# A decoder layer on one core: other column cuts for the last output tile, and other engines for two of four modulation sums

## The chip, the cores and the metric

One core of one Trainium2 chip runs the program; the seven others are idle. The metric is the device time of one execution in microseconds, lower is better. Five engines work side by side, each through its own instructions in order: TensorE (PE in the profile, PEld for its weight loads), VectorE (DVE), ScalarE (ACT), GpSimd (POOL) and SyncE (SP, which here only issues DMAs). They wait for each other through semaphores.

## The reference

A layer over 256 tokens of width 1024, batch 1. What matters here is its first and its last step:

```python
mod = c @ w_ada[layer] + b_ada[layer]
shift, scale, gate = jnp.split(mod, 3, axis=-1)
h = x * (1.0 + scale[:, None, :]) + shift[:, None, :]
proj = h @ w_in[layer]
...
y = jnp.concatenate([o_a, o_b], axis=-1) @ w_out[layer]
x = _layernorm(DEEPNORM_ALPHA * x + gate[:, None, :] * y, ln_g[layer], ln_b[layer])
```

`c` is one vector of 1024, `w_ada` is 1024 x 3072, `w_in` 1024 x 4096, `w_out` 1024 x 1024, all float32. Between the two steps lie two kinds of attention over eight heads each, each gated by a SiLU branch.

## The kernel before

**How the order comes about.** The kernel first records operations (`op`, with engine, assumed duration, what is read and written) in a plan. `Plan.emit` then plays the plan forward with its assumed costs, and each engine takes whatever is ready and due first. So the order on each engine is a result of the assumed durations, and an edit at one place can move instructions elsewhere. On the chip each engine keeps that order and waits wherever an operand is late.

**The modulation (`modulate`, lines 393 to 443).** `mod = c @ w_ada` needs, for each of 2048 columns (shift and scale; gate is made later), a sum over 1024 rows of `w_ada`. The rows are laid out as 128 partitions times eight rows j, so the work is first eight weighted additions, acc = acc + c[j] * row j, over 512 columns each, and then one sum across the partitions. The columns come in four pairs g = 0 to 3 (`GROUPS`); pair g gives shift and scale of the x tiles 2g and 2g + 1, tile k being 128 of the 1024 features. The kernel before does this in three ways:

- Pair 0: all eight additions on VectorE (lines 412 and 415), then the sum across partitions as matmuls of acc against a column of ones (line 423, two tiles times shift and scale, each of them in two passes), which leaves the result in the wanted layout.
- Pairs 1 and 2 (`pag=[1, 2]`): rows 0 to 3 go through TensorE, as products with `cz`, a tile that holds c[j] in one column of 32 (line 406, four products with 512 columns each, into one PSUM buffer). VectorE then adds rows 4 to 7, the first of them onto that PSUM buffer. The sum across partitions is a product with 32 columns of ones (line 432), a COPY to SBUF by VectorE (line 436) and a transpose on TensorE (line 437).
- Pair 3: all eight additions on VectorE, then lines 432 to 437.

Two small additions of the bias give `md` (line 440), and `make_h` forms h = x * (1 + scale) + shift for the tile: `hH` is its high part in float32r, `hL` the rest (for the first tile of a pair `hH` comes from VectorE, line 450; for the second from ScalarE).

**The projections.** x is transposed on TensorE tile by tile (line 387) and copied out by ScalarE into `xT`. Each 128-row block of the weights is split into a high part (`whi`, ScalarE, line 270) and a low part (`wlo`, VectorE, line 275). A product is three matmuls: hH with whi, hL with whi, hH with wlo (line 296 is the helper that records nearly every matmul). `proj1(k)` does this for x tile k and the first 1792 columns of `w_in`: 36 matmuls, 30 of 256 and 6 of 512 columns. It can only begin when hH of tile k is there. Nine further sets of columns follow, with the attention in between.

**The output.** Products with `w_out` for token tile t go into PSUM pieces `CUTS[t]`: two of 512 columns for t = 0, and 512, 384 and 128 columns for t = 1. Each piece gets 24 matmuls (eight contraction blocks times three parts). Two of the eight blocks of t = 1 are done early, in a fill stretch (`fill`, nf = 2); the other six come piece by piece at the very end. `layer_norm(1)` follows: for each piece an addition of x (line 275) and statistics (line 743) on VectorE, then their aggregate, the power -0.5 on GpSimd, two normalising steps and three output DMAs.

**Loads.** SyncE issues all loads in the order of `LOADS`, through 11 raw buffers; the eight row blocks of a pair (a10 to a13 for pair 1) are eight DMAs.

Of the kernel before, what the change touches and what calls it, by code (L numbers as in the profile page):

```python
# [237 lines left out]
def hybrid_kernel(ctx: ExitStack, tc: tile.TileContext, x, c, w_in, w_out, w_ada, b_ada, ln_g, ln_b,  # L238
# [154 lines left out]
    md = {}  # L393

    def modulate(g):

        tiles = GROUPS[g]
        n = 128 * len(tiles)
        acc = P.buf("acc", [128, 2, n])
        a = [T["ada", g, j] for j in range(8)]  # L400
        d = 2 * n / 0.96 + 128
        if g in CFG["pag"]:

            pa = P.buf("ps", [128, 2, n])
            for j in range(4):
                pe(n * 0.977, lambda j=j: nc.tensor.matmul(  # L406
                    pa.ap[32 * j:32 * j + 32], cz[:, j], a[j][0](), start=True, stop=True, skip_group_check=True), a[j][1] + ["cz"], [(pa, 0)], 512)
            pe_end()
        for j in range(4 if g in CFG["pag"] else 0, 8):
            src, rd = a[j][0], a[j][1] + ["c"]  # L410
            if j == 0:
                op(DVE, n / 0.96 + 133, lambda src=src: nc.vector.tensor_scalar(acc.ap, src(), cc[:, 0:1], None, op0=OP.mult),
                   rd, [(acc, 0)], p2=True)
                continue
            op(DVE, d, lambda src=src, j=j: nc.vector.scalar_tensor_tensor(  # L415
                acc.ap, src(), cc[:, j:j + 1], pa.ap if j == 4 and g in CFG["pag"] else acc.ap, op0=OP.mult, op1=OP.add),
                rd + [(pa, 0) if j == 4 and g in CFG["pag"] else (acc, 0)], [(acc, 0)], p2=j > 4)
        if g not in CFG["colsum"]:
            pm = P.buf("ps", [128, len(tiles), 2])
            for q, k in enumerate(tiles):  # L420
                cs = slice(q * 128, q * 128 + 128)
                for s in range(2):
                    pe(205, lambda q=q, s=s, cs=cs: nc.tensor.matmul(pm.ap[:, q, s:s + 1], acc.ap[:, s, cs], ones[:, 0:1],  # L423
                       start=True, stop=True, skip_group_check=True), [(acc, 0)], [(pm, 1)], 4)
            pe_end()
            col = lambda q: pm.ap[:, q]
        else:

            pm, z = P.buf("ps", [128, 2, 128]), P.buf("md", [128, 128])
            for s in range(2):  # L430
                for q in range(2):
                    pe(50, lambda r=64 * s + 32 * q, s=s, cs=slice(q * 128, q * 128 + 128): nc.tensor.matmul(  # L432
                        pm.ap[r:r + 32, 0], ones[:, 0:32], acc.ap[:, s, cs], start=True, stop=True, skip_group_check=True),
                       [(acc, 0)], [(pm, 0)], 128)
# [523 lines left out]
```

## Time and profile before

| | us |
|---|---|
| three timed runs | 163.99, 164.50, 165.16 |
| median | 164.50 |
| the profiled execution | 164.21 |
| its span in the trace | 162.4 |
| TensorE busy | 152.6 |
| VectorE busy | 136.9 |
| ScalarE busy | 96.2 |

The profile is one execution. The span runs from the first to the last instruction that the trace holds; the profiled execution's own time is 1.8 us longer. A matmul's end in the trace is modelled and overlaps the next one, so its price is read from the distance between starts, not from its duration. A line in the code can be that of a helper: 270, 275 and 296 stand for many operations, which are told apart by the names of what they write and read. Times in views are counted from the start of the span.

### The profile page before, as it was taken

Reading aid. Unit: us, or ns where it says so; the run is one execution under the profiler, and the core shown is the slowest. Engines: PE = TensorE matmul, PEld = TensorE weight load, DVE = VectorE, ACT = ScalarE, POOL = GpSimd, SP = SyncE. Lnnn points to the kernel's source line nnn. Section 1 sums busy time; section 2 is a strip of 40 time slices with the busy share of each in tenths; the row PEclk is TensorE's granted clock in tenths of the full one; section 3 lists DMA queues with packets and bytes.
Section 4 is the critical chain, followed back from the end, with each engine's and each line's share of the span. In section 5 each row is a group of like instructions: output and inputs, shape, how many; then the busy total and the mean of one; then the engine's idle time right before and its main releaser. Section 6 shows DMA issues by size and latency. Waiting matters only on the chain.

```text
span 162.4 us, 3296 instructions
## 1 busy us (share of the span) xinstructions
PE 152.6 (94%) x1192; PEld 132.1 (81%) x1192; DVE 136.9 (84%) x313; ACT 96.2 (59%) x243; POOL 3.1 (2%) x9
## 2 busy tenths in 40 slices
PE   6998998999999999999999999999999999999920
PEld 2447976789988999997998999899799978888920
DVE  2687668686999979999999899999999999828672
ACT  3008608406788798447999999952589991503000
POOL 3000000000000000000000000000000000001020
PEclk9999999999999999999999999999999999999975
DMA  5999999999999999997457839700199700000303
GB/s 147 272 388 387 349 387 362 361 402 359 369 401 357 348 348 348 349 346 235 137 178 224 281 118 348 277 4 0 17 328 404 288 4 4 0 0 0 129 0 129
DMA packets 25405, 38.11 MB, mean 235 GB/s; under 512 B 1681, under 2 KB 20141, under 8 KB 25390
## 3 DMA queue, kind: packets, MB, share of 16 engines
q1 hardware_dynamic: 25066, 37.76, 68.0%
q8 instruction: 9, 0.15, 0.4%
q10 hardware_dynamic: 324, 0.15, 0.3%
q14 instruction: 6, 0.05, 0.1%
HBM read 36.85 MB, written 1.05 MB: 233 GB/s over the span
## 4 chain that ended last, share of the span: by engine, by line
PE 93%; DVE 3%; issue 1%; DVEq 0%
PE ps L296 79%; PE ps L792 6%; PE ps L677 3%; PE ps L387 1%; PE ps L406 1%; DVE raw L765 1%; PE ps L432 1%; PE ps L423 1%; DVE hH L450 1%; DVE raw L760 0%; DVE wlo L275 0%; PE ps L556 0%; DVE md L275 0%; DVEq L954 0%; DVE bn L743 0%
## 5 line engine op out<-in xcount | busy, mean ns | idle before, releaser
L270 ACT ACTIVATE whi<-raw 128x512 fp32r<-128x512 f32 (+1 forms) x83 | 45.8, 610 | 30.3 <-DMA raw<-in_w_in_dram 18.7
L275 DVE TENSOR_TENSOR wlo<-raw,whi 128x512 fp32r<-128x512 f32 (+1 forms) x83 | 51.6, 665 | 1.0 <-ACT whi L270 0.7
L296 PE MATMUL ps<-hH,whi 128*128 128x256 f32 x192 | 46.1, 290 | 1.4 <-DVE hH L450 1.3
L296 PE MATMUL ps<-hH,wlo 128*128 128x256 f32 x192 | 45.4, 285 | 0.0
L296 PE MATMUL ps<-hL,whi 128*128 128x256 f32 x192 | 44.7, 284 | 0.0
L296 PEld LDWEIGHTS ps<-hH,whi 128*128 128x128 f32 x192 | 33.2, 190 | 4.5 <-issue 2.3
L296 PEld LDWEIGHTS ps<-hH,wlo 128*128 128x128 f32 x192 | 33.4, 190 | 1.7 <-issue 1.0
L296 PEld LDWEIGHTS ps<-hL,whi 128*128 128x128 f32 x192 | 33.0, 190 | 1.0 <-issue 0.4
L415 DVE SCALAR_TENSOR_TENSOR acc<-raw,cc,acc 128x512 f32<-128x512 f32 x20 | 15.0, 752 | 2.0 <-DMA raw<-in_w_ada_dram 1.4
L296 PE MATMUL ps<-whi,hH 128*128 128x256 f32 (+1 forms) x48 | 15.8, 332 | 0.0
L296 PE MATMUL ps<-whi,hL 128*128 128x256 f32 (+1 forms) x48 | 15.3, 321 | 0.0
L657 ACT ACTIVATE prob<-z,st 128x128 f32<-128x128 f32 (+1 forms) x32 | 14.2, 448 | 1.8 <-DVE st L654 1.8
L296 PE MATMUL ps<-wlo,hH 128*128 128x256 f32 (+1 forms) x48 | 15.2, 320 | 0.0
L296 PE MATMUL ps<-whi,ogh 128*128 128x512 f32 (+2 forms) x40 | 14.4, 359 | 0.0
L296 PE MATMUL ps<-wlo,ogh 128*128 128x512 f32 (+2 forms) x40 | 14.3, 357 | 0.0
L296 PE MATMUL ps<-whi,ogl 128*128 128x512 f32 (+2 forms) x40 | 14.3, 356 | 0.0
L272 ACT ACTIVATE prob<-prob,st 128x128 f32<-128x128 f32 (+1 forms) x32 | 12.3, 444 | 0.4 <-DVE st L662 0.4
L548 DVE SCALAR_TENSOR_TENSOR gate<-raw,cc,gate 128x512 f32<-128x512 f32 x16 | 11.2, 739 | 0.7 <-DMA raw<-in_w_ada_dram 0.7
L792 PE MATMUL ps<-warm 128*128 128x512 bf16 x36 | 10.5, 446 | 1.3 <-DVE warm L311 1.3
L275 DVE TENSOR_TENSOR pp<-ps,rope_t 128x512 f32<-128x512 f32 x16 | 10.3, 682 | 1.1 <-PE ps L296 1.1
L296 PEld LDWEIGHTS ps<-whi,hH 128*128 128x128 f32 x48 | 9.0, 190 | 1.1 <-issue 0.7
L270 ACT ACTIVATE pt<-ps 128x384 f32<-128x384 f32 x16 | 7.4, 487 | 3.6 <-PE ps L677 3.5
(84 smaller groups left out, 184.2 us busy)
## 6 DMA issues: line engine op xcount, KB each, us to landing
raw<-in_w_in_dram SPq DMA_DIRECT2D x26, 512.0 KB, 8.0
raw<-in_w_ada_dram SPq DMA_DIRECT2D x32, 256.0 KB, 7.2
raw<-in_w_ada_dram SPq DMA_DIRECT2D x8, 512.0 KB, 4.5
raw<-in_w_out_dram SPq DMA_DIRECT2D x8, 512.0 KB, 7.6
raw<-in_w_in_dram SPq DMA_DIRECT2D x8, 384.0 KB, 7.5
out_dram<-raw SPq DMA_DIRECT2D x3, 256.0 KB, 2.0
xs<-in_x_dram SPq DMA_DIRECT2D x1, 512.0 KB, 6.7
gate<-gate_row SPq DMA_DIRECT2D x1, 512.0 KB, 4.4
```

The source lines that it names most:

```text
L270: op(ACT, dur, lambda: nc.scalar.activation(o(), i(), AF.Copy), r, w)
L272: op(ACT, dur, lambda: nc.scalar.activation(o(), i(), AF.Copy, scale=scale()), r, w)
L275: op(e, dur, lambda: vec[e].tensor_tensor(o(), a(), b(), alu), r, w, p2=p2)
L296: f = lambda: nc.tensor.matmul(o(), a(), b(), start=start, stop=stop, skip_group_check=True)
L387: pe(107, lambda t=t: nc.tensor.transpose(b.ap[:, t * 128:(t + 1) * 128], xs[:, t, k * 128:(k + 1) * 128], ident), [("x", 0 if k == 0 else ...
L406: pe(n * 0.977, lambda j=j: nc.tensor.matmul(pa.ap[32 * j:32 * j + 32], cz[:, j], a[j][0](), start=True, stop=True, skip_group_check=True) ...
L415: op(DVE, d, lambda src=src, j=j: nc.vector.scalar_tensor_tensor(acc.ap, src(), cc[:, j:j + 1], pa.ap if j == 4 and g in CFG["pag"] else a ...
L423: pe(205, lambda q=q, s=s, cs=cs: nc.tensor.matmul(pm.ap[:, q, s:s + 1], acc.ap[:, s, cs], ones[:, 0:1], start=True, stop=True, skip_group ...
L548: op(DVE, 663, lambda cs=cs: nc.vector.scalar_tensor_tensor(gate[:, cs], b.ap[:, cs], cc[:, r:r + 1], gate[:, cs], op0=OP.mult, op1=OP.add ...
L657: op(ACT, n * 0.833 + 280, lambda e=e, t=t, i=i, c=c: nc.scalar.activation(p[e].ap[:, c], z[e].ap[:, c], AF.Exp, bias=st.ap[:, i:i + 1], s ...
L677: pe(109, lambda i=i: nc.tensor.transpose(b.ap[:, i * 128:(i + 1) * 128], p.ap[:, i * 128:(i + 1) * 128], ident), [(p, 1 if i else 0)], [( ...
L792: op(PE, 216, lambda: nc.tensor.matmul(pw.ap, warm[:, 0:128], warm, start=True, stop=True), [], [(pw, 0)], due=1e8)
```

## The change

Three edits, and what the planner makes of them.

1. Token tile 1's output is cut into 512, 256 and 256 columns. The planner's assumed cost of a narrow matmul gets a floor of 112 ns.
2. Pairs 0 and 1 (`one=[0, 1]`): the eighth addition is done in two halves, one for each x tile, and the matmuls with the column of ones of a tile wait for their half alone. Pair 1 now takes the way of pair 0: all eight additions on VectorE and no products with `cz`.
3. Only pair 2 keeps products on TensorE, for rows 2 to 5 (`PROWS`). Their PSUM buffer is no longer added to by VectorE: ScalarE copies it to SBUF (`pas`), VectorE adds rows 0, 1, 6 and 7 by itself, and the products with ones take in both tiles, eight in place of four, accumulating in PSUM.

```diff
-CFG = dict(colsum=[1, 2, 3], pag=[1, 2], ...
+PROWS = (2, 3, 4, 5)
+CFG = dict(one=[0, 1], colsum=[2, 3], pag=[2], ...
...
+        rows = [j for j in range(8) if g not in CFG["pag"] or j not in PROWS]
+        def on_pe():
             pa = P.buf("ps", [128, 2, n])
-            for j in range(4):
+            for i, j in enumerate(PROWS):
...
+            o = P.buf("pas", [128, 2, n])
+            copy(lambda: o.ap, lambda: pa.ap, acost(512, True), [(pa, 0)], [(o, 0)])
+            return o
...
+            parts = [(q, slice(q * 128, q * 128 + 128)) for q in range(2)] if j == 7 and g in CFG["one"] else [(None, slice(0, n))]
+            for q, cs in parts:
...
+            if j == 1 and g in CFG["pag"]:
+                sums = [(on_pe(), 0)] + sums
...
-                       start=True, stop=True, skip_group_check=True), [(acc, 0)], [(pm, 1)], 4)
-            pe_end()
+                       start=True, stop=True, skip_group_check=True), [(acc, q)], [(pm, q)], 4)
+                if q or g in CFG["one"]:
+                    pe_end()
...
-            for s in range(2):
+            for i, (x, _) in enumerate(sums):
+                for s in range(2):
...
-    CUTS = (((0, 512), (512, 1024)), ((0, 512), (512, 896), (896, 1024)))
+    CUTS = (((0, 512), (512, 1024)), ((0, 512), (512, 768), (768, 1024)))
...
-                mm((c1 - c0) / 2.2 + 2, [(o, i), (w, c0 // 512), "late"], [(b, 0)], lambda b=b: b.ap,
+                mm(max((c1 - c0) / 2.2 + 2, 112), [(o, i), (w, c0 // 512), "late"], [(b, 0)], lambda b=b: b.ap,
```

VectorE around pair 1, before. `acc` is the running sum, `raw` the loaded rows, `ps_315` the products with cz, `wlo` low parts of weights, and the hH that ends the piece is that of x tile 2.

```order
L275 TENSOR_TENSOR wlo_276<-raw_148,whi_267 128x512 x2
L275 TENSOR_TENSOR wlo_290<-raw_151,whi_280 128x512
L275 TENSOR_TENSOR wlo_290<-raw_151,whi_280 128x256
L415 SCALAR_TENSOR_TENSOR acc_323<-raw_171,cc,ps_315 128x512
L415 SCALAR_TENSOR_TENSOR acc_323<-raw_171,cc,acc_323 128x512
L415 SCALAR_TENSOR_TENSOR acc_323<-raw_179,cc,acc_323 128x512 x2
L436 COPY md_369<-ps_362 128x128
L275 TENSOR_TENSOR wlo_373<-raw_188,whi_359 128x512
L275 TENSOR_TENSOR md_380<-ps_362,bcol 128x2
L275 TENSOR_TENSOR md_382<-ps_362,bcol 128x2
L450 TENSOR_SCALAR hH<-xT,md_380 128x256
```

The same place of VectorE after the change.

```order
L276 TENSOR_TENSOR wlo_279<-raw_148,whi_270 128x512 x2
L421 TENSOR_SCALAR acc_294<-raw_155,cc 128x512
L427 SCALAR_TENSOR_TENSOR acc_294<-raw_155,cc,acc_294 128x512
L427 SCALAR_TENSOR_TENSOR acc_294<-raw_163,cc,acc_294 128x512 x2
L427 SCALAR_TENSOR_TENSOR acc_294<-raw_171,cc,acc_294 128x512 x2
L427 SCALAR_TENSOR_TENSOR acc_294<-raw_179,cc,acc_294 128x512
L427 SCALAR_TENSOR_TENSOR acc_294<-raw_179,cc,acc_294 128x2x128 x2
L276 TENSOR_TENSOR wlo_358<-raw_151,whi_284 128x512
L276 TENSOR_TENSOR wlo_358<-raw_151,whi_284 128x256
L276 TENSOR_TENSOR md_369<-ps_355,bcol 128x2
L276 TENSOR_TENSOR md_371<-ps_355,bcol 128x2
L465 TENSOR_SCALAR hH<-xT,md_369 128x256
```

Eight additions stand where four stood, the last one in two halves. They begin two splits earlier, and those two low parts (of the second weight block of x tile 1) now follow the sums; COPY is gone.

ScalarE around x tile 4, before. `whi_441` belongs to tile 3, `whi_512` and `whi_542` to tile 4; `ps_515` and `ps_528` are the transposed x tiles 4 and 5.

```order
L270 ACTIVATE whi_441<-raw_293 128x512
L270 ACTIVATE whi_441<-raw_293 128x256
L270 ACTIVATE whi_512<-raw_338 128x512
L270 ACTIVATE xT<-ps_515 128x256
L452 ACTIVATE h_524<-xT,md_507 128x256
L270 ACTIVATE whi_512<-raw_338 128x512
L270 ACTIVATE xT<-ps_528 128x256
L270 ACTIVATE whi_542<-raw_345 128x512
```

The same place of ScalarE after the change; `whi_452` belongs to tile 3, `whi_520` and `whi_548` to tile 4.

```order
L271 ACTIVATE whi_452<-raw_297 128x512
L271 ACTIVATE whi_452<-raw_297 128x256
L271 ACTIVATE pas_481<-ps_469 128x512
L271 ACTIVATE whi_520<-raw_346 128x512
L271 ACTIVATE xT<-ps_522 128x256
L467 ACTIVATE h_533<-xT,md_514 128x256
L271 ACTIVATE xT<-ps_535 128x256
L271 ACTIVATE whi_520<-raw_346 128x512
L271 ACTIVATE whi_548<-raw_360 128x512
```

The copy of pair 2's products is new, and the copy of x tile 5 now stands ahead of the second half of tile 4's first weight block.

VectorE around pair 3's end, before. `acc_564` holds pair 3's sums, `ps_654` their column sums; hH is that of x tile 6.

```order
L415 SCALAR_TENSOR_TENSOR acc_564<-raw_457,cc,acc_564 128x512 x2
L275 TENSOR_TENSOR wlo_606<-raw_357,whi_573 128x512
L275 TENSOR_TENSOR wlo_659<-raw_433,whi_602 128x512
L436 COPY md_669<-ps_654 128x128
L275 TENSOR_TENSOR wlo_659<-raw_433,whi_602 128x256
L275 TENSOR_TENSOR wlo_677<-raw_470,whi_652 128x512
L275 TENSOR_TENSOR md_687<-ps_654,bcol 128x2
L275 TENSOR_TENSOR md_689<-ps_654,bcol 128x2
L450 TENSOR_SCALAR hH<-xT,md_687 128x256
```

The same place of VectorE after the change.

```order
L427 SCALAR_TENSOR_TENSOR acc_570<-raw_474,cc,acc_570 128x512 x2
L276 TENSOR_TENSOR wlo_612<-raw_373,whi_580 128x512
L451 COPY md_670<-ps_661 128x128
L276 TENSOR_TENSOR wlo_674<-raw_437,whi_608 128x512
L276 TENSOR_TENSOR md_683<-ps_661,bcol 128x2
L276 TENSOR_TENSOR md_685<-ps_661,bcol 128x2
L276 TENSOR_TENSOR wlo_674<-raw_437,whi_608 128x256
L465 TENSOR_SCALAR hH<-xT,md_683 128x256
```

One split stands between the sums and the COPY where two stood. Between the COPY and hH there is one split of 512 and one of 256 columns as before, the narrow one now behind `md`. On TensorE the products of pair 2 with `cz` move from x tile 2's matmuls into x tile 3's, with eight products with ones behind them, and pair 3's column sums stand three matmuls later.

## Rows read from the trace of the kernel before

**Rows 1.** The page's part 4: the chain that ended last, share by engine.

```profile
PE 93%; DVE 3%; issue 1%; DVEq 0%
```

**Rows 2.** The chain in order of time: start, length, engine and line.

```profile
11.88 1.00 PE ps L423 x8
...
20.42 0.99 PE ps L406 x8
...
25.03 0.40 PE ps L432 x8
...
50.90 28.70 PE ps L296 x262
```

**Rows 3.** Timeline of PE, 127 to 156 us: start, length, what.

```profile
127.93 0.28 PE L296 MATMUL ps<-hH,wlo 128*128 128x256 f32 x1
128.05 0.28 PE L296 MATMUL ps<-hH,whi 128*128 128x256 f32 x1
...
138.05 0.33 PE L296 MATMUL ps<-whi,ogh 128*128 128x384 f32 x1
...
138.85 0.45 PE L296 MATMUL ps<-whi,ogh 128*128 128x512 f32 x1
139.15 0.40 PE L296 MATMUL ps<-wlo,ogh 128*128 128x512 f32 x1
139.38 0.40 PE L296 MATMUL ps<-whi,ogl 128*128 128x512 f32 x1
...
150.07 0.33 PE L296 MATMUL ps<-whi,ogh 128*128 128x384 f32 x1
...
153.21 0.22 PE L296 MATMUL ps<-whi,ogh 128*128 128x128 f32 x1
...
155.06 0.27 PE L296 MATMUL ps<-whi,ogl 128*128 128x128 f32 x1
```

**Rows 4.** Timeline of DVE, 153 to 157 us.

```profile
153.41 0.56 DVE L275 TENSOR_TENSOR raw<-ps,xs 128x384 f32<-128x384 f32 x1 [1.34 <-PE ps L296]
...
155.37 0.29 DVE L275 TENSOR_TENSOR raw<-ps,xs 128x128 f32<-128x128 f32 x1 [0.81 <-PE ps L296]
...
156.03 0.24 DVE L754 BATCH_NORM_AGGREGATE mv<-bn 128x2 f32<-128x18 f32 x1
```

**Rows 5.** Groups by form on DVE, 150 to 162.4 us: busy us, mean ns.

```profile
L765 DVE SCALAR_TENSOR_TENSOR raw<-raw,mv,raw 128x256 f32<-128x256 f32 x2 | 0.9, 481 | 0.0
```

**Rows 6.** Timeline of PE at three earlier places.

```profile
1.34 2.31 PE L792 MATMUL ps<-warm 128*128 128x512 bf16 x5 [1.34 <-DVE warm L311]
...
27.08 0.71 PE L296 MATMUL ps<-hH,whi 128*128 128x256 f32 x4 [0.67 <-DVE hH L450]
...
121.66 0.69 PE L677 MATMUL ps<-ident,prob 128*128 128x128 f32 x3
```

**Rows 7.** Timeline of DVE, 11 to 52 us.

```profile
17.20 2.23 DVE L275 TENSOR_TENSOR wlo<-raw,whi 128x512 fp32r<-128x512 f32 x4
...
22.34 2.33 DVE L415 SCALAR_TENSOR_TENSOR acc<-raw,cc,acc 128x512 f32<-128x512 f32 x3
...
26.32 0.23 DVE L275 TENSOR_TENSOR md<-ps,bcol 128x2 f32<-128x2 f32 x2
...
49.01 0.29 DVE L436 COPY md<-ps 128x128 f32<-128x128 f32 x1
...
50.34 0.41 DVE L450 TENSOR_SCALAR hH<-xT,md 128x256 fp32r<-128x256 f32 x1
```

**Rows 8.** Timeline of ACT, around 39 and 121 us.

```profile
38.94 0.61 ACT L270 ACTIVATE whi<-raw 128x512 fp32r<-128x512 f32 x1
39.46 0.36 ACT L270 ACTIVATE xT<-ps 128x256 f32<-128x256 f32 x1
...
121.08 1.48 ACT L272 ACTIVATE prob<-prob,st 128x128 f32<-128x128 f32 x4
```

**Rows 9.** Busy us (instructions) by window: PE, PEld, DVE, ACT, POOL; PEclk, DMA share, GB/s.

```profile
24.00:28.00 4.00, 3.33 (x29) 2.69 (x29) 3.22 (x9) 3.12 (x7) 0.00 (x0) 1.00 1.07 366
```

More of the change, by code (lines that the diff above doesn't have):

```diff
@@ L29 @@
     "a30 a31 w51 a32 a33 w60 w61 w70 w71").split()]
-CFG = dict(colsum=[1, 2, 3], pag=[1, 2], empty=2000, beh=[], look=0.3, ahead=0, raw=11, hl=6, a0=-4.0, ra=0.7, rb=0.7, s0=1, s1=5, nf=2,
+PROWS = (2, 3, 4, 5)
+CFG = dict(one=[0, 1], colsum=[2, 3], pag=[2], empty=2000, beh=[], look=0.3, ahead=0, raw=11, hl=6, a0=-4.0, ra=0.7, rb=0.7, s0=1, s1=5, nf=2,
            pvo=[1, 0], pe0=1280, lock=1, sact=[2, 6],
@@ L251, in hybrid_kernel @@
     P.pool(wts, "wlo", CFG["hl"])
-    for tg, n in (("acc", 2), ("h", 2), ("md", 4), ("pp", 2), ("rot", CFG["nrot"]), ("z", CFG["nz"]),
+    for tg, n in (("acc", 2), ("pas", 1), ("h", 2), ("md", 4), ("pp", 2), ("rot", CFG["nrot"]), ("z", CFG["nz"]),
                   ("st", CFG["nst"]), ("prob", CFG["nprob"]), ("pt", CFG["pt"]), ("og", 2), ("bn", 2), ("mv", 2)):
@@ L401, in modulate @@
         d = 2 * n / 0.96 + 128
-        if g in CFG["pag"]:
+        qs = [(acc, q) for q in range(2)]
+        rows = [j for j in range(8) if g not in CFG["pag"] or j not in PROWS]
+        def on_pe():
             pa = P.buf("ps", [128, 2, n])
-            for j in range(4):
-                pe(n * 0.977, lambda j=j: nc.tensor.matmul(
-                    pa.ap[32 * j:32 * j + 32], cz[:, j], a[j][0](), start=True, stop=True, skip_group_check=True), a[j][1] + ["cz"], [(pa, 0)], 512)
+            for i, j in enumerate(PROWS):
+                pe(n * 0.977, lambda i=i, j=j: nc.tensor.matmul(
+                    pa.ap[32 * i:32 * i + 32], cz[:, i], a[j][0](), start=True, stop=True, skip_group_check=True), a[j][1] + ["cz"], [(pa, 0)], 512)
             pe_end()
-        for j in range(4 if g in CFG["pag"] else 0, 8):
+            o = P.buf("pas", [128, 2, n])
+            copy(lambda: o.ap, lambda: pa.ap, acost(512, True), [(pa, 0)], [(o, 0)])
+            return o
+        sums = [(acc, 0)]
+        for j in rows:
             src, rd = a[j][0], a[j][1] + ["c"]
@@ L412, in modulate @@
                 op(DVE, n / 0.96 + 133, lambda src=src: nc.vector.tensor_scalar(acc.ap, src(), cc[:, 0:1], None, op0=OP.mult),
[L413 removed]
+                   rd, qs, p2=True)
                 continue
[L415 to L417 removed]
+            parts = [(q, slice(q * 128, q * 128 + 128)) for q in range(2)] if j == 7 and g in CFG["one"] else [(None, slice(0, n))]
+            for q, cs in parts:
+                w = qs if q is None else [qs[q]]
+                op(DVE, d if q is None else 395, lambda src=src, j=j, cs=cs: nc.vector.scalar_tensor_tensor(
+                    acc.ap[:, :, cs], src()[:, :, cs], cc[:, j:j + 1], acc.ap[:, :, cs], op0=OP.mult, op1=OP.add), rd + w, w, p2=True)
+            if j == 1 and g in CFG["pag"]:
+                sums = [(on_pe(), 0)] + sums
         if g not in CFG["colsum"]:
@@ L429, in modulate @@
             pm, z = P.buf("ps", [128, 2, 128]), P.buf("md", [128, 128])
-            for s in range(2):
[L431 to L434, printed above, removed]
+            for i, (x, _) in enumerate(sums):
+                for s in range(2):
+                    for q in range(2):
+                        pe(50, lambda r=64 * s + 32 * q, s=s, x=x, i=i, cs=slice(q * 128, q * 128 + 128): nc.tensor.matmul(
+                            pm.ap[r:r + 32, 0], ones[:, 0:32], x.ap[:, s, cs], start=i == 0, stop=i == len(sums) - 1,
+                            skip_group_check=True), [(x, 0)] + qs, [(pm, 2)], 128)
             pe_end()
-            op(DVE, 205, lambda: nc.vector.tensor_copy(z.ap, pm.ap[:, 0]), [(pm, 0)], [(z, 0)])
-            op(PE, 112, lambda: nc.tensor.transpose(pm.ap[:, 1], z.ap, ident), [(z, 0)], [(pm, 1)], cols=128)
+            op(DVE, 205, lambda: nc.vector.tensor_copy(z.ap, pm.ap[:, 0]), [(pm, 2)], [(z, 0)])
+            op(PE, 112, lambda: nc.tensor.transpose(pm.ap[:, 1], z.ap, ident), [(z, 0)], [(pm, 0), (pm, 1)], cols=128)
             col = lambda q: pm.ap[:, 1].rearrange("p (s q r) -> p q s r", s=2, q=2)[:, q, :, 0]
@@ L442, in modulate @@
                lambda k=k: bcol.rearrange("p (s k) -> p k s", k=8)[:, k, 0:2],
-               OP.add, 71, [(pm, 1), "bcol"], [(m, 0)], False)
+               OP.add, 71, [(pm, q), "bcol"], [(m, 0)], False)
     def make_h(k):
```

2 lines of the change are left out of this document (1 added, 1 removed).

## Prediction

> **What bounds the kernel now.** I read the chain of waits first: 93% of it is TensorE [rows 1], so time is lost or won where TensorE works or waits. The chain in order of time then says where it does both. From 50.90 us TensorE follows itself without a break [rows 2], and so it goes, in all pieces, to 155.35; before that it works between short waits for the modulation sums (lines 406, 423 and 432). Two stretches are touched: the start, up to 50.90, and the end, from the first piece of token tile 1 at 138 us to the last output. Between them the change alters orders only, not work.
>
> TensorE's timeline gives the price of a matmul as the distance to the next start [rows 3]. 128x256 float32r costs 0.12 (127.93 to 128.05, and several hundred like it). In the last block the 18 pieces of 384 columns take 153.21 - 150.07 = 3.14, so 0.174 each; the 18 of 128 columns take 1.85 from 153.21 to the last start at 155.06, so 0.109. A third of the columns costs nearly two thirds of the time: the narrow piece is the expensive one.
>
> **The end.** All 24 matmuls of 384 and 24 of 128 columns become 48 of 256. Six of each product group stand in the fill: 138.05 to 138.85 is 0.80, and the 512 matmul behind them waits 0.30 for its successor (138.85 to 139.15) where the next waits 0.23 (139.15 to 139.38). After: 6 x 0.12 = 0.72 and no such extra. Saved: 0.15, twice (contraction blocks 0 and 1): -0.31. In the last block 36 x 0.12 = 4.32 from 150.07; the last start moves from 155.06 to 154.27: -0.79. That is all on the path, since nothing but TensorE stands there.
>
> Behind the last matmul VectorE adds x and takes the statistics. The last piece is now 256 wide. The add took 0.29 for 128 columns and 0.56 for 384 [rows 4], so 0.42 for 256; add and statistics together ran from 155.37 to 156.03, 0.66, and I take 0.92 for 256: +0.26. From the last matmul's start to the add it was 0.31, I take 0.34: +0.03. The middle piece's add and statistics (0.85) lie beside 18 x 0.12 = 2.16 of TensorE work and are free. The end: -0.31 - 0.79 + 0.26 + 0.03 = **-0.81**. Its bounds: were 256 columns as dear here as 384, 48 x 0.054 = 2.6 worse; as cheap as 128, 0.5 better. The value stands by the row of the very shape.
>
> [...]
>
> **The start, pair 0.** The eighth sum in halves costs 0.48 for each half (the row of the same operation on 128x256, [rows 5]), the second about 0.4 behind the first, so the sum ends 0.1 later; but the first half's four passes of line 423, half of the 1.00 in [rows 2], run during the second half's sum. x tile 0 starts some 0.3 earlier. I count it 0: the next wait, for pair 1, takes it.
>
> **Pair 1.** Removed from TensorE between 19 and 27 us: the products with cz (0.99), the column sums (0.40) [rows 2], and with luck the wait of 0.67 at 27.08 [rows 6]. Added: 1.00 for sums with a ones column. On VectorE eight sums stand where four stood. In the order they follow two of four splits: 17.20 + 2 x 0.56 = 18.35 [rows 7]. A sum costs 0.78 (2.33 for three); the first one, without an addend, less: seven end at about 23.7. The last data is no limit, since the kernel before began that sum at 22.34 + 2 x 0.78 = 23.9 without waiting. Halves: 24.2 and 24.6. TensorE meanwhile runs out of work: tile 1 began six matmuls (0.83) ahead of 20.42 [rows 2], at 19.6, and 28 of its 36, 24 of 256 and 4 of 512 columns, need nothing of pair 1's sums or of what is queued behind them: 19.6 + 24 x 0.12 + 4 x 0.23 = 23.4. It waits 0.8; its eight passes end at about 25.2. What is queued behind the sums on VectorE: the two low parts of the second weight block (1.0), which TensorE needs right after the passes, then md, then hH. So md starts at about 25.65 instead of 26.32 and tile 2 at 26.4 instead of 27.08: a lead of 0.7. Bounds: 1.2 if no wait is left, 0 if the sums come 0.7 later.
>
> **Pair 2.** The products with cz stay (0.99), now in tile 3 instead of tile 2, and four more column sums come: +0.40. The ScalarE copy costs between 0.36 (128x256, at 39.46) and 0.61 (128x512, at 38.94) [rows 8] and lies beside hL products; uncovered it would cost just that. Lead at tile 4: 0.7 - 0.4 = 0.3. Does tile 4 find its operands? The order on ScalarE puts the copy of the fifth transposed x tile ahead of the second half of tile 4's high weights. Before, that half began at 38.94 and the copy at 39.46 took 0.27 of the engine; now it begins at about 39.2 and TensorE has only four matmuls and two transposes to do before it needs it. So the lead shrinks to 0.2 to 0.3.
>
> **Pair 3** is late next. VectorE does its eight sums as before, and hH begins at 50.34 [rows 7]; TensorE starts tile 6 on it at 50.90 [rows 2]. The order moves the COPY of the column sums ahead by one split (0.6), but the COPY at 49.01 needs the column sums, which stand three matmuls later on TensorE. I take a gain of 0.15; bounds 0.6 better, 0.3 worse. So the start: **-0.15**, whatever the lead was before: of the 0.7 won at pair 1 most is given back at tiles 4 and 6.
>
> Sum: -0.81 - 0.15 = -0.96. The profiled execution took 164.21 (its span 162.4 and 1.8 around it); the three timed runs have a median 0.3 above it, 164.5. I start midway, from 164.36, and forecast **163.4**, 0.6% below.
>
> **Rivals.** (a) *The lead survives.* If pair 3's hH comes with TensorE, 0.7 to 1.0 of what pair 1 wins stays: -0.81 - 0.85, 162.7. For it: the COPY moves ahead by 0.6. Against: VectorE's sums for pair 3 end where they did, and nothing on that engine between 41 and 49 us is taken away. 0.19.
> (b) *A new wait in the attention, slower than before.* At 121 us TensorE's transposes follow ScalarE closely: four scalings run from 121.08 to 122.56 [rows 8], and three transposes that need them start at 121.66 and spread over 0.69 [rows 6]. Attention tiles are scheduled anew; the order puts an exponential ahead of a copy of transposed probabilities there. Two exponentials of about 0.6 ahead of what TensorE waits for would cost 1.2: -0.96 + 1.2 = +0.24, 164.6, slower than before. It decides from 1.0 of such a wait on. For it: this is the one close place after 50.90. Against: only neighbours are swapped. 0.08.
> (c) *The clock falls.* TensorE now waits 0.8 before pair 1's passes and again before tile 2. What the lower level costs stands at the start: five warm-up matmuls of 512 columns took 2.31 [rows 6], 0.46 each, against 0.23 for as many columns at 139.15. So each us at 1.2 GHz loses half a us, and five of them from 24 us on would cost 2.5: -0.81 + 2.5, 166.05. It is slower than before once the clock is down for 2 us. Against: with idle of 0.67 in it, 24 to 28 us was granted 1.00 [rows 9]. 0.03.
> (d) *The width makes no difference.* If the 0.11 of a narrow matmul belonged to something that stays, the end would be +0.29 and the time 164.36 + 0.29 - 0.15 = 164.5. Against: it shows in the fill and in the last block alike. 0.03.
>
> **How the numbers follow.** The forecast has 0.63, (a) 0.19, (b) 0.08, (c) 0.03, (d) 0.03; 0.04 is left for the spread of the runs (163.99 to 165.16). A measurement of this kernel tells about 1% from no change, so 162.85 and 166.15 are the lines. Half of (a) and about a sixth of the forecast's own spread lie below: 0.2. Above lie half of (c) and a little of (b): 0.04. The rest, 0.76, is within 1%. The likeliest case's own range is 162.7 to 164.0; for 8 in 10, with (a), (b) and the bounds of the start, 162.3 to 164.7.
>
> **What would show it.** Right: the last add on VectorE 4.5 behind the start of the last block of matmuls instead of 5.3 (150.07 to 155.37), 0.12 between all matmuls of the last two pieces; tile 2 near 26.4, tile 4 within 0.4 and tile 6 within 0.3 of before. Wrong: another spacing than 0.12 in the last block; tile 6 starting before 50.4 (then (a)); any wait of TensorE after 51 us, above all near 121 (then (b)); a granted clock below 1.00 before 155 (then (c)).

## Result: 1.0% faster, inside the range, with a larger gain than forecast

| | before | after |
|---|---|---|
| median of four timed runs, us | 164.70 | 163.03 |
| lowest and highest | 163.99, 165.16 | 162.52, 163.18 |
| the profiled execution | 164.21 | 163.18 |
| its span | 162.4 | 161.4 |
| TensorE busy | 152.6 | 151.2 |
| VectorE busy | 136.9 | 138.8 |

The ratio is 0.9896, with a 95% interval of 0.9853 to 0.9940: 1.0 to 2.4 us less, where 0.96 was forecast. A second comparison of the same two kernels gave 0.9877 (0.9831 to 0.9922), 163.01 against 164.75. The forecast time of 163.4 was close, the forecast gain too small. Since the loads do not arrive equally early in every execution, the profiles are read below as distances between two events, not as times from the start.

**The end.** The timeline of TensorE after the change, to be held against [rows 3]:

```profile
137.88 0.28 PE L297 MATMUL ps<-whi,ogh 128*128 128x256 f32 x1
...
138.83 0.40 PE L297 MATMUL ps<-wlo,ogh 128*128 128x512 f32 x1
...
149.55 0.28 PE L297 MATMUL ps<-whi,ogh 128*128 128x256 f32 x1
...
153.74 0.28 PE L297 MATMUL ps<-whi,ogl 128*128 128x256 f32 x1
```

And that of VectorE at the end, which answers to [rows 4]:

```profile
154.06 0.42 DVE L276 TENSOR_TENSOR raw<-ps,xs 128x256 f32<-128x256 f32 x1 [1.27 <-PE ps L297]
...
154.98 0.24 DVE L769 BATCH_NORM_AGGREGATE mv<-bn 128x2 f32<-128x18 f32 x1
```

From the first narrow piece in the fill to the second matmul of 512 columns it takes 138.83 - 137.88 = 0.95, before it was 139.15 - 138.05 = 1.10: -0.15, twice. In the last block 35 steps take 153.74 - 149.55 = 4.19, so 0.120 each. From the last block's first matmul to the last add it is 154.06 - 149.55 = 4.51 instead of 5.30: -0.79. Add and statistics take 0.92 instead of 0.66: +0.26. The end gives -0.31 - 0.79 + 0.26 = -0.84.

**The start.** The timeline of VectorE shows pair 0's sums as one row. Before the change:

```profile
7.00 4.76 DVE L415 SCALAR_TENSOR_TENSOR acc<-raw,cc,acc 128x512 f32<-128x512 f32 x6 [0.57 <-DMA raw<-in_w_ada_dram]
```

After it, with what follows up to x tile 6:

```profile
7.30 4.82 DVE L427 SCALAR_TENSOR_TENSOR acc<-raw,cc,acc 128x512 f32<-128x512 f32 x7 [1.01 <-DMA raw<-in_w_ada_dram]
...
13.13 0.41 DVE L465 TENSOR_SCALAR hH<-xT,md 128x256 fp32r<-128x256 f32 x1
...
18.96 0.48 DVE L421 TENSOR_SCALAR acc<-raw,cc 128x512 f32<-128x512 f32 x1
19.48 5.61 DVE L427 SCALAR_TENSOR_TENSOR acc<-raw,cc,acc 128x512 f32<-128x512 f32 x8
...
48.97 0.29 DVE L451 COPY md<-ps 128x128 f32<-128x128 f32 x1
...
50.31 0.41 DVE L465 TENSOR_SCALAR hH<-xT,md 128x256 fp32r<-128x256 f32 x1
```

I count from the start of pair 0's eighth sum. Before, that is the last of six in the row, and it takes 0.76: 7.00 + 4.76 - 0.76 = 11.00. After, it is the first of the two halves, which together take 0.88: 7.30 + 4.82 - 0.88 = 11.24. Three rows of TensorE from before go with [rows 2] and [rows 6], the first matmuls of x tiles 0, 1 and 4:

```profile
13.73 0.83 PE L296 MATMUL ps<-hH,whi 128*128 128x256 f32 x5 [0.63 <-DVE hH L450]
...
19.35 0.72 PE L296 MATMUL ps<-hH,whi 128*128 128x256 f32 x4
...
39.46 0.54 PE L296 MATMUL ps<-hH,whi 128*128 128x256 f32 x3
```

After the change the same stretch of TensorE reads:

```profile
13.69 1.19 PE L297 MATMUL ps<-hH,whi 128*128 128x256 f32 x8 [0.20 <-DVE hH L465]
...
15.19 0.60 PE L388 MATMUL ps<-ident,xs 128*128 128x128 f32 x4
...
19.72 0.72 PE L297 MATMUL ps<-hH,whi 128*128 128x256 f32 x4
...
24.84 1.02 PE L436 MATMUL ps<-ones,acc 128*128 128x1 f32 x8 [0.61 <-DVE acc L427]
...
26.69 1.19 PE L297 MATMUL ps<-hH,whi 128*128 128x256 f32 x8
...
39.23 0.66 PE L297 MATMUL ps<-hH,whi 128*128 128x256 f32 x4
...
40.14 0.73 PE L297 MATMUL ps<-hH,whi 128*128 128x256 f32 x4
...
50.87 0.71 PE L297 MATMUL ps<-hH,whi 128*128 128x256 f32 x4
```

Against the eighth sum, tile 2 starts at 15.45 instead of 16.08 (27.08 - 11.00), a lead of 0.63; tile 4 at 27.99 instead of 28.46 (39.46 - 11.00), 0.47; and tile 6 at 39.63 instead of 39.90 (50.90 - 11.00). The start gives -0.27.

**Between them.** From tile 6's first matmul to the first piece of 384 or 256 columns it takes 137.88 - 50.87 = 87.01, before it was 138.05 - 50.90 = 87.15: -0.14. The sum of the three is -1.25. The two profiled executions differ by 1.03 only, since pair 0's eighth sum came 0.24 later in the second one.

### The profile page after: what moved, and what is told of

Its sections match the earlier page's. It is cut to its first block, busy times and chain, and to the rows that moved or that the text cites. A ratio compares the mean times of both kernels' runs of the same rounds, so it can differ in the third digit from the quotient of the medians.

```text
span 161.4 us, 3299 instructions
## 1 busy us (share of the span) xinstructions
PE 151.2 (94%) x1191; PEld 131.7 (82%) x1191; DVE 138.8 (86%) x318; ACT 96.5 (60%) x244; POOL 3.2 (2%) x9
## 4 chain that ended last, share of the span: by engine, by line
PE 82%; DVE 9%; DMA 3%; ACT 1%; issue 1%; SPq 1%; DVEq 0%
PE ps L297 75%; DVE acc L427 6%; PE ps L692 3%; DMA raw<-in_w_ada_dram 3%; PE ps L436 1%; SPq L340 1%; DVE wlo L276 1%; DVE raw L780 1%; PE ps L388 1%; PE ps L410 1%; PE ps L447 1%; DVE raw L775 0%; ACT xT L271 0%; PE ps L571 0%; ACT whi L271 0%
## 5 line engine op out<-in xcount | busy, mean ns | idle before, releaser
L297 PE MATMUL ps<-hH,whi 128*128 128x256 f32 x192 | 45.6, 291 | 0.2 <-DVE hH L465 0.2
L297 PE MATMUL ps<-hH,wlo 128*128 128x256 f32 x192 | 44.7, 285 | 0.0
L297 PEld LDWEIGHTS ps<-hH,whi 128*128 128x128 f32 x192 | 32.7, 191 | 3.8 <-issue 1.4
L297 PEld LDWEIGHTS ps<-hL,whi 128*128 128x128 f32 x192 | 33.5, 191 | 0.8 <-DVE hL L276 0.2
L297 PEld LDWEIGHTS ps<-hH,wlo 128*128 128x128 f32 x192 | 32.9, 190 | 0.9 <-DVE wlo L276 0.2
L427 DVE SCALAR_TENSOR_TENSOR acc<-raw,cc,acc 128x512 f32<-128x512 f32 (+1 forms) x26 | 18.3, 710 | 2.0 <-DMA raw<-in_w_ada_dram 1.4
L297 PE MATMUL ps<-whi,hH 128*128 128x256 f32 (+1 forms) x48 | 15.1, 332 | 0.0
L297 PE MATMUL ps<-whi,ogh 128*128 128x512 f32 (+1 forms) x40 | 14.0, 350 | 0.0
L297 PE MATMUL ps<-wlo,ogh 128*128 128x512 f32 (+1 forms) x40 | 13.9, 348 | 0.0
L297 PE MATMUL ps<-whi,ogl 128*128 128x512 f32 (+1 forms) x40 | 13.9, 347 | 0.0
```

Source lines behind the costliest of these rows:

```text
L297: f = lambda: nc.tensor.matmul(o(), a(), b(), start=start, stop=stop, skip_group_check=True)
L427: op(DVE, d if q is None else 395, lambda src=src, j=j, cs=cs: nc.vector.scalar_tensor_tensor(acc.ap[:, :, cs], src()[:, :, cs], cc[:, j:j ...
```

## Experiments

Each kernel is compared with the kernel before on its own chip.

**1. The new cuts alone (`cuts_only`).** The kernel before with this edit and the floor of 112 ns:

```diff
-    CUTS = (((0, 512), (512, 1024)), ((0, 512), (512, 896), (896, 1024)))
+    CUTS = (((0, 512), (512, 1024)), ((0, 512), (512, 768), (768, 1024)))
```

> The kernel before with edit 1 alone (512, 256 and 256 columns). Theory, the two ends of the program add up: the start is as before (tile 2 at 27.1, tile 6 at 50.9 us), 0.12 between matmuls of the last two pieces, last block to last add 4.5 instead of 5.3, in all 0.8 us below the kernel before. Rival, the measured 1.7 between the medians comes from here alone: 1.4 to 1.7 below. Rival, width makes no difference: 0.3 above.

Measured: 163.88 against 164.47, ratio 0.996 (0.9932 to 0.9988). From the first product with w_out to the end of the span it takes 29.8 us as in the changed kernel; the kernel before takes 30.7. The timed runs give the end 0.2 to 1.1 by itself (0.6 by the medians), the trace 0.9; the whole gain, 1.7 by the medians, it is not. In its profiled execution TensorE ran partly at the lower clock around 16 us, so its rows up to tile 6 are 1.6 later and not compared (last section).

**2. The start alone (`start_only`).** The changed kernel with the cuts and the cost of before.

> The changed kernel with the old cuts (512, 384 and 128 columns), so edits 2 and 3 alone. Theory, the lead of pair 1 is given back: tile 2 some 0.4 earlier than before, tile 6 at 50.9 as before, 0 to 0.2 us below the kernel before. Rival, the lead survives up to the end: 0.85 below, tile 6 before 50.4.

Measured: 163.95 against 164.47, ratio 0.9959 (0.9939 to 0.9979). That is 0.3 to 1.0 us, more than the 0.15 forecast and the 0 to 0.2 expected here. Its profile has tile 6's hH at 39.10 behind the eighth sum (39.34 before), and 81.28 from there to the first product with w_out (81.42 before): the lead of 0.6 at tile 2 does shrink to 0.24, so the rival falls as a mechanism, but the rest of the way is shorter too. By the medians the end alone gains 0.6 and the start alone 0.5, together 1.1.

**3. Two pieces of 512 columns (`two_pieces`).**

```diff
-    CUTS = (((0, 512), (512, 1024)), ((0, 512), (512, 896), (896, 1024)))
+    CUTS = (((0, 512), (512, 1024)), ((0, 512), (512, 1024)))
```

> The kernel before with token tile 1 cut in two pieces of 512. Theory, a matmul costs its columns (0.44 to 0.46 ns each) from 256 columns up: 18 x 0.2275 = 4.1 in the last block against 4.3 for twice 256, but 512 columns to add and take statistics of behind the last matmul (1.4 instead of 0.92), so 0.2 to 0.3 us slower than the kernel with the new cuts alone, 0.55 below the kernel before. Rival, each matmul has a fixed price of its own of 0.05 and more: then 36 matmuls fewer save more than the wider tail costs, 1.3 below the kernel before.

Measured: 163.68 against 164.47, ratio 0.9959 (0.9936 to 0.9981). The time from the first product with w_out to the end is 0.7 shorter than before, against 0.87 with 256 columns: the second cut is worth about 0.15, less than expected and too little for the timed runs to tell. A last piece of 256 columns gains 0.5 behind TensorE (add and statistics take 0.92 instead of 1.45), of which two thirds are paid back on it.

**4. A piece of 64 columns (`cut_64`).** As above with (512, 960) and (960, 1024).

> The kernel before with pieces of 512, 448 and 64 columns. Theory, a matmul of this kind has a floor of 0.11 however narrow: 64 columns cost 0.109 to 0.112, 448 cost 0.20, the last block is 18 x 0.31 = 5.6 instead of 5.0 and the time 0.7 to 0.8 us above the kernel before. Rival, below 128 columns time falls with the columns (64 cost 0.055): 0.6 below. Rival, a line through 128 and 256 columns (0.104 for 64): 0.6 above, to be told from the floor by the spacing alone.

Measured: 164.97 against 164.47, ratio 1.0044 (1.0019 to 1.0070). TensorE's timeline, last piece:

```profile
153.97 0.19 PE L296 MATMUL ps<-whi,ogh 128*128 128x64 f32 x1
154.00 0.27 PE L296 MATMUL ps<-wlo,ogh 128*128 128x64 f32 x1
...
155.78 0.28 PE L296 MATMUL ps<-whi,ogl 128*128 128x64 f32 x1
```

From the second start on, 16 steps take 1.78, 0.111 each, just as with 128 columns. There is a floor, and a line through 128 and 256 columns (0.104) is out. The time rose by 0.5 by the medians (0.3 to 1.2) and by 0.44 in the rows from the first product with w_out on, instead of 0.7 to 0.8: 448 columns cost 0.20 as expected, but the first matmul of a narrow piece is followed after 0.03, which the expectation counted as 0.11, in both fill groups and in the last block.

**5. Weights of 64 tokens (`half_rows`).** The kernel before; in the last piece the six late blocks use half of the stationary operand (the one that is loaded as weights ahead of each matmul), so that six of eight blocks are left out there for 64 of the 128 tokens.

```diff
...
-                   lambda o=o: (ogh["t"] if o == "ogh" else ogl)[:, i, t * 128:(t + 1) * 128],
+                   lambda o=o, p=p: (ogh["t"] if o == "ogh" else ogl)[:, i, t * 128:t * 128 + p],
...
```

> The kernel before (512, 384 and 128 columns); in the last piece the 18 late matmuls take weights of 64 tokens instead of 128 (the other 64 tokens miss six of eight blocks there). Theory, loading 128 x 128 weights sets the floor of a narrow matmul: the spacing falls from 0.11 towards 0.06, the last block is 0.9 shorter and the time 0.9 below the kernel before. Rival, the floor is a fixed price of each matmul: 0.11 still, no gain.

Measured: 163.85 against 164.55, ratio 0.9964 (0.9926 to 1.0002). The same piece on TensorE:

```profile
153.31 0.22 PE L296 MATMUL ps<-whi,ogh 128*64 128x128 f32 x1
...
154.33 0.22 PE L296 MATMUL ps<-whi,ogl 128*64 128x128 f32 x1
```

The starts are 0.060 apart, so 17 steps take 1.02 instead of 1.85. With as many columns moving and half as many weight columns the price fell to nearly half, so the floor of 0.11 is not a price of the instruction. Half as many weight columns are half as many output rows too, and this run does not part the two. The weight loads themselves speak for the load, first of 128 columns (`cut_64`), then of 64 (`half_rows`):

```profile
154.08 0.19 PEld L296 LDWEIGHTS ps<-whi,ogl 128*128 128x128 f32 x1
```

```profile
153.43 0.14 PEld L296 LDWEIGHTS ps<-whi,ogh 128*64 128x64 f32 x1
```

A load is 0.05 shorter, and so is the step from one matmul to the next. The timed interval reaches just beyond 1; the verdict rests on the rows.

**6. Pair 0 in halves alone (`pair0_halves`).** The kernel before, with the eighth sum of pair 0 split:

```diff
...
+            if g == 0 and j == 7:
+                for q in range(2):
...
```

> The kernel before with one thing of edit 2: pair 0's eighth sum in two halves, each half's passes on its own. Theory after the first four runs: hH of x tile 0 starts 1.9 behind the start of the last whole sum instead of 2.17, and as everything up to tile 6 hangs on it, hH of tile 6 comes 0.27 earlier too (39.07 behind the last whole sum instead of 39.34): 0.25 to 0.3 below the kernel before. The recorded forecast: the 0.3 is taken by the next wait, 0.

Measured: 164.91 against 164.75, ratio 1.0004 (0.9974 to 1.0034). No gain, as the prediction had it. Its VectorE and TensorE rows show where the 0.27 won by the halves went. VectorE:

```profile
11.15 0.88 DVE L418 SCALAR_TENSOR_TENSOR acc<-raw,cc,acc 128x256 f32<-128x256 f32 x2
...
50.73 0.41 DVE L456 TENSOR_SCALAR hH<-xT,md 128x256 fp32r<-128x256 f32 x1
```

TensorE:

```profile
13.61 1.19 PE L296 MATMUL ps<-hH,whi 128*128 128x256 f32 x8 [0.20 <-DVE hH L456]
...
15.11 0.60 PE L387 MATMUL ps<-ident,xs 128*128 128x128 f32 x4
...
19.62 0.72 PE L296 MATMUL ps<-hH,whi 128*128 128x256 f32 x4
...
27.49 0.71 PE L296 MATMUL ps<-hH,whi 128*128 128x256 f32 x4 [0.79 <-DVE hH L456]
```

Tile 0 starts 2.46 behind the eighth sum (13.61 - 11.15) instead of 2.73 (13.73 - 11.00), but tile 2 16.34 (27.49 - 11.15) instead of 16.08, and tile 6's hH comes 39.58 behind it instead of 39.34. The planner has now put the transposes of x tile 1 behind ten matmuls instead of six. From tile 0's first matmul to tile 1's it takes 19.62 - 13.61 = 6.01, where it took 19.35 - 13.73 = 5.62: the 0.27 is lost there and more. Another 0.13 goes because one more matmul of tile 1 stands ahead of the products with cz. The changed kernel has the same transposes behind ten matmuls (15.19) and the same stretch, 19.72 - 13.69 = 6.03.

**7. Pair 3 relieved (`pair3_short`).** The changed kernel, same order; pair 3's eighth sum covers 2 of 256 features.

```diff
-            parts = [(q, slice(q * 128, q * 128 + 128)) for q in range(2)] if j == 7 and g in CFG["one"] else [(None, slice(0, n))]
+            parts = [(q, slice(q * 128, q * 128 + 128)) for q in range(2)] if j == 7 and g in CFG["one"] else [(None, slice(0, 2 if (g, j) == (3, 7) else n))]
```

> The changed kernel, in the same order, with pair 3's eighth sum over 2 of 256 features (the eighth row of the others is left out): VectorE is 0.65 ahead before the column sums of pair 3. Theory of the forecast, VectorE's eight sums hold tile 6: hH of tile 6 comes 0.2 to 0.6 earlier, up to 0.25 below the changed kernel (TensorE has no more wait than that there). Rival, the place of the column sums in TensorE's own order and the splits between COPY and hH hold it: hH of tile 6 within 0.1 of the changed kernel (37.2 behind hH of tile 0), no gain.

Measured: 163.19 against 164.75, ratio 0.9883 (0.9833 to 0.9934), the changed kernel beside it 163.01. VectorE:

```profile
45.06 2.58 DVE L427 SCALAR_TENSOR_TENSOR acc<-raw,cc,acc 128x512 f32<-128x512 f32 x4
...
48.92 0.29 DVE L451 COPY md<-ps 128x128 f32<-128x128 f32 x1 [0.67 <-PE ps L447]
...
50.26 0.41 DVE L465 TENSOR_SCALAR hH<-xT,md 128x256 fp32r<-128x256 f32 x1
```

The four sums take 2.58 instead of 3.11, and the COPY then waits 0.67 for TensorE's column sums. Tile 6's hH stands 37.17 behind tile 0's, against 37.18 in the changed kernel. VectorE's sums do not hold tile 6. The COPY waits for the column sums at their place in TensorE's order, and the 1.34 from the COPY to hH are VectorE's work between them.

**8. Two orders mended (`both_orders`).** The transposes of x tile 1 go back behind six matmuls, and the second half of tile 4's first weight block goes ahead of the copy of x tile 5. The edit adds dependencies that only the planner sees:

```diff
...
+    P.ops[T["xt", 5] + 1][3].update((T["wop", 4, 0], T["wop", 4, 0] + 1))
+    for i in range(6, 36):
+        P.ops[T["p1", 0] + i][3].add(T["xt", 1])
...
```

> The changed kernel with two orders mended: x tile 1 is transposed after 6 matmuls of tile 0 instead of 10, and the second half of tile 4's first weight block goes ahead of the copy of x tile 5 on ScalarE. Theory: the sums of pair 1 start 0.5 earlier, the wait of 0.6 ahead of pair 1's passes goes, tile 2 and tile 4 come 0.4 to 0.5 earlier, and tile 6 follows TensorE: 0.3 to 0.5 below the changed kernel. Rival, tile 6 is held by VectorE and by pair 3's rows: the lead is lost there and the time is that of the changed kernel.

Measured: 162.99 against 164.75, ratio 0.988 (0.9831 to 0.9929): the time of the changed kernel. VectorE:

```profile
7.48 4.82 DVE L428 SCALAR_TENSOR_TENSOR acc<-raw,cc,acc 128x512 f32<-128x512 f32 x7 [0.34 <-DMA raw<-in_w_ada_dram]
...
18.56 0.48 DVE L422 TENSOR_SCALAR acc<-raw,cc 128x512 f32<-128x512 f32 x1
...
23.37 1.67 DVE L428 SCALAR_TENSOR_TENSOR acc<-raw,cc,acc 128x512 f32<-128x512 f32 x3 [0.39 <-DMA raw<-in_w_ada_dram]
...
50.30 0.41 DVE L466 TENSOR_SCALAR hH<-xT,md 128x256 fp32r<-128x256 f32 x1
```

TensorE:

```profile
13.88 0.83 PE L297 MATMUL ps<-hH,whi 128*128 128x256 f32 x5 [0.19 <-DVE hH L466]
...
19.50 0.72 PE L297 MATMUL ps<-hH,whi 128*128 128x256 f32 x4
```

From tile 0's first matmul to tile 1's it takes 5.62 again (19.50 - 13.88). Pair 1's sums start 7.14 behind the eighth sum (7.48 + 4.82 - 0.88 = 11.42) instead of 7.72, but then wait 0.39 for their last rows: the loads are the next limit there. Tile 6's hH is 0.2 earlier (38.88 against 39.07). The 0.2 is lost again between tile 6 and w_out, where the planner ordered the attention anew (81.6 instead of 81.3; TensorE's transposes near 125 us are spread out there).

**9. The changed kernel again (`changed_again`).**

> The changed kernel itself, on the same chip as the others. If its parts add up: 0.87 from the end, 0.27 from pair 0, up to 0.2 from the attention, in all 1.1 to 1.4 us below the kernel before; if the first comparison's medians hold, 1.7.

Measured: 163.01 against 164.75, ratio 0.9877 (0.9831 to 0.9922), with the rows of the first profile within 0.05. That is 1.3 to 2.8 us; the 1.25 that the rows give lies just below it and inside the first comparison's interval.

**10. The attention order alone (`att_later`).** The kernel before; in the planner one group of transposes is held back until one more matmul is placed.

```diff
...
+    P.hold = {T["tr", "b", 4]: T["tr", "b", 4] + 9}
...
```

> The kernel before with the attention order of the changed kernel: the transposes near 121 us stand one matmul later on TensorE (two later ones one earlier), the five ScalarE steps around them as there. Theory: TensorE's wait at these transposes goes, from hH of tile 6 to the last transposes it takes 76.4 us where the four undisturbed profiles of the old order have 76.4, 76.5, 76.8 and 77.1: 0.15 to 0.35 us below the kernel before. Rival, the wait comes back at the next transposes: 0.

Measured: 164.58 against 164.55, ratio 1.0002 (0.9976 to 1.0028). In its profile the wait is gone: 81.30 from tile 6's hH to the first product with w_out. The timed runs show nothing of it, and bound it at 0.4 us. So it is a difference that the traces show and the clock cannot; how much of it is in the changed kernel's time stays open.

**11. Pair 2 as before (`pair2_old`).** The changed kernel; pair 2 in the way of before.

```diff
...
-            o = P.buf("pas", [128, 2, n])
-            copy(lambda: o.ap, lambda: pa.ap, acost(512, True), [(pa, 0)], [(o, 0)])
-            return o
+            return pa
...
```

> The changed kernel with pair 2 in the way of the kernel before (rows 0 to 3 with cz, VectorE adds the rest onto PSUM, four column sums). Theory, pair 2's new way costs TensorE 0.2 to 0.4 that later waits take anyway: hH of tile 4 0.2 to 0.5 earlier than in the changed kernel, tile 6 within 0.1, the time within 0.2. Rival, the new way is what brings the gain at tile 6 (VectorE relieved of one wait): tile 6 0.26 later and the time 0.3 above the changed kernel.

Measured: 163.62 against 164.55, ratio 0.9931 (0.9907 to 0.9954). Timed runs of the changed kernel's order have medians of 163.01 to 163.16. VectorE:

```profile
7.21 4.82 DVE L427 SCALAR_TENSOR_TENSOR acc<-raw,cc,acc 128x512 f32<-128x512 f32 x7 [0.72 <-DMA raw<-in_w_ada_dram]
...
45.00 3.11 DVE L427 SCALAR_TENSOR_TENSOR acc<-raw,cc,acc 128x512 f32<-128x512 f32 x4
49.23 0.29 DVE L449 COPY md<-ps 128x128 f32<-128x128 f32 x1
50.56 0.41 DVE L463 TENSOR_SCALAR hH<-xT,md 128x256 fp32r<-128x256 f32 x1
```

TensorE near 121 us:

```profile
121.98 0.84 PE L690 MATMUL ps<-ident,prob 128*128 128x128 f32 x3
```

Counted from the eighth sum (7.21 + 4.82 - 0.88 = 11.15), tile 4's hH is 0.1 later than in the changed kernel, not earlier, and tile 6's 0.34 later (39.41). Pair 3's sums end at the same distance (36.96 against 36.99), but the COPY stands 0.35 later, behind two splits as before the change. So the rival held for tile 6, though not for its reason: pair 2 itself gains next to nothing by the new way, but the planner orders pair 3 better with it. The time of this kernel carries more than that. In its profile the transposes near 121 us spread over 0.84, where the changed kernel's take 0.49, and from tile 6's hH to the first product with w_out it takes 81.68 instead of 81.28. The 0.5 to 0.6 in the timed runs is not the price of pair 3's order alone.

**12. Idle time ahead of tile 0 (`short_warm`).** The changed kernel, same order, the last three warm-up matmuls one column wide.

```diff
-        op(PE, 216, lambda: nc.tensor.matmul(pw.ap, warm[:, 0:128], warm, start=True, stop=True), [], [(pw, 0)], due=1e8)
+        op(PE, 216, lambda m=512 if w < CFG["warm"] - 3 else 1: nc.tensor.matmul(pw.ap[:, 0:m], warm[:, 0:128], warm[:, 0:m], start=True, stop=True), [], [(pw, 0)], due=1e8)
```

> The changed kernel, in the same order, with the last three warm-up matmuls one column wide, so that TensorE is idle for 0.8 instead of 0.2 ahead of tile 0's first matmul. Theory: this idle time is what lets the granted clock fall (in the profile of the kernel with the new cuts alone it was 0.94 and 0.63, and 0.70 to 0.50 were granted from 14 to 18 us): the same fall here, in all or some executions, tile 2 1 to 1.7 later and the time as much above the changed kernel. Rival, the clock does not fall after 0.8: the time of the changed kernel.

Measured: 163.16 against 164.55, ratio 0.9916 (0.9885 to 0.9947). TensorE's first matmul of tile 0, and a stretch of its table (start and end, length, busy time of TensorE, its weight loads, VectorE, ScalarE and GpSimd, then the granted clock, the share of DMA and GB/s):

```profile
13.56 1.19 PE L297 MATMUL ps<-hH,whi 128*128 128x256 f32 x8 [0.79 <-DVE hH L465]
```

```profile
16.00:18.00 2.00, 2.00 (x15) 1.90 (x16) 0.81 (x2) 1.97 (x5) 0.00 (x0) 1.00 1.10 350
```

The idle time is there, the clock stays at 1.00 (in the stretch before, 14 to 16 us, as well), and the median does not move. The rival held.

## Why the prediction was right, and where its size was off

**The end: right in every term.** 0.12 between all matmuls of the last two pieces; -0.31 in the fill, -0.79 in the last block, +0.26 behind it, all as worked out; only the 0.03 from the last matmul to the add did not appear (154.06 - 153.74 = 0.32, before 0.31). Experiment 1 shows it standing alone, experiments 4 and 5 show why the step "the narrow piece is the expensive one" holds: with 128 weight columns a matmul of 64 or 128 columns costs 0.11, and 128 columns by themselves need no more than 0.06. Rival (d) is out. The Trainium skill, "TensorE: Matmul & The Clock Gate", section "LDWEIGHTS (loading the stationary operand)", prices the load at the weight's columns divided by 1.2, in ns: 107 for 128 and 53 for 64 (estimates from that page). The traces agree, with steps of 111 and 60 ns.

**Pair 0: right, for another reason.** "The next wait, for pair 1, takes it": alone it gained nothing. What took it was not a wait that stood there already but the order: the transposes of x tile 1 went from behind six to behind ten matmuls, and TensorE's tile 0 took 6.0 instead of 5.62. With the transposes back at their place it is 5.62 (experiment 8). The prediction did not read that row of the new order. Whether its wait would have taken the 0.3 in the old order, no run shows.

**Pair 1: right within 0.1.** The sums were to begin at 18.35 (the terms given add up to 18.32), 7.35 behind the eighth sum, and began 7.72 behind it, since tile 1 came later by the same transposes; their last half ended 0.25 later than worked out, but md only 0.06. The wait ahead of the passes was 0.61 where 0.8 stood. The lead at tile 2 is 0.63, forecast 0.7. The granted clock stayed at 1.00, as in [rows 9], so rival (c) did not happen:

```profile
24.00:28.00 4.00, 3.39 (x24) 2.93 (x24) 3.96 (x11) 2.81 (x6) 0.00 (x0) 1.00 1.07 362
```

**Pair 2 and tile 4: right in the end, with one term too large.** The ScalarE copy took 0.60 and lay beside TensorE's work. The lead was to fall to 0.3 and fell to 0.47, since the four more column sums cost 0.22 where 0.40 stood: all eight took 0.57 (35.89 to 36.46), the four before 0.35 (35.77 to 36.12). But the half of tile 4's first weight block that stands behind the copy of x tile 5 cost TensorE another 0.2, as the order on ScalarE had said, which leaves 0.27:

```profile
39.19 0.38 ACT L271 ACTIVATE xT<-ps 128x256 f32<-128x256 f32 x1
39.47 1.45 ACT L271 ACTIVATE whi<-raw 128x512 fp32r<-128x512 f32 x3
```

**Pair 3 and tile 6: the term of -0.15 was too small.** It measured -0.27. Rival (a), the whole lead, did not come. But the reason given against it, that nothing is taken from VectorE between 41 and 49 us, does not hold: taking 0.5 away there changed nothing (experiment 7). What counts is what the prediction named beside it, the COPY one split earlier and the column sums at their place on TensorE. In experiment 11 the COPY stands 0.35 later and tile 6's hH 0.34 later when that split returns.

**The attention: a term that was missing.** Rival (b) looked at the right place with the wrong sign. The order moved the transposes near 121 us behind one more matmul, and the wait that the kernel before had there vanished. In the profiles of its order (leaving out the one at the lower clock) the way from tile 6's hH to w_out takes 81.2 to 82.0; in the order of the changed kernel 81.25 to 81.4, five profiles. The same three transposes in `pair0_halves`, whose order there is that of before:

```profile
122.48 0.84 PE L683 MATMUL ps<-ident,prob 128*128 128x128 f32 x3 [0.23 <-ACT prob L272]
```

And after the change, with no wait:

```profile
121.79 0.49 PE L692 MATMUL ps<-ident,prob 128*128 128x128 f32 x3
```

Before, in the profile on which the prediction rests, they spread over 0.69 [rows 6]. That profile shows 0.14 of this; others show up to 0.7, or nothing. Experiment 10 could not find it in the timed runs.

The sum by rows is 1.25 instead of 0.96: 0.12 more at the start, 0.14 in the attention, 0.03 at the end. The mis-sized step is the start's "I take a gain of 0.15"; the missing one is that "between them the change alters orders only" was taken to mean no gain. The timed runs say 1.0 to 2.4, in the second comparison 1.3 to 2.8, and in that of `short_warm`, which has the same order, 0.9 to 1.9. What they show beyond 1.25 is not assigned; the end and the start alone gave 0.6 and 0.5 by their medians (experiments 1 and 2).

## What to carry to other kernels

Read the price of a matmul from the distance between starts, by shape, before cutting an output: with 128 weight columns a piece of 64 columns cost as much here as one of 128, and two pieces of 256 were cheaper than one of 384 and one of 128. Where a planner sets the order, an edit's own work is only half of it: look at what the new order does to the neighbours (here four transposes, one split, one matmul ahead of a group of transposes), since these moved the start by as much as the edits did. A lead won early in a chain of stages is worth what the last stage with a wait of its own leaves of it; here 0.63 became 0.27.

## What was not expected of the hardware

The floor of a narrow float32r matmul followed the weight's columns closely: 0.111 for 128, 0.060 for 64, while 64 moving columns cost the same 0.11 as 128. One moving column does too: the eight passes with the column of ones in the changed kernel take 25.75 - 24.84 = 0.91 up to the next matmul's start.

The profile of `cuts_only` shows the granted clock falling to its lower level for a while at the start, in stretches as above:

```profile
14.00:16.00 2.00, 2.00 (x12) 1.93 (x13) 2.00 (x5) 1.24 (x4) 0.00 (x0) 0.70 1.02 378
16.00:18.00 2.00, 2.00 (x11) 1.90 (x10) 0.92 (x3) 1.97 (x5) 0.00 (x0) 0.50 1.09 355
```

0.50 is 1.2 of 2.4 GHz. TensorE had been idle for 0.94 ahead of pair 0's passes and for 0.63 ahead of tile 0 just before, and tile 6's hH came 1.55 later against the eighth sum than in the kernel before. In the fall matmuls of 256 columns started 0.213 apart instead of 0.12. By rival (c)'s price, half a us for each us at the lower level, the missing shares of the clock (18 to 20 us had 0.95) would cost (0.30 + 0.50 + 0.05) x 2 = 1.7. The 0.46 of a warm-up matmul behind that price was read from the length of a row; from start to start they are 0.43 apart. The kernel before has the 0.63 in its own profile, without the 0.94 and without a fall. No fall came either with 0.79 ahead of tile 0 (experiment 12), with 0.53 and 0.63 (`att_later`), or with 0.88 and 0.20 (`pair0_halves`). What lets the clock fall there stays open.
